# A hybrid decoder step: the gate tiles go through DRAM, and TensorE's order has their products earlier

## The chip, the cores and the metric

The kernel runs on one core of a Trainium2 chip. The core has TensorE (PE, matrix products into PSUM), VectorE (DVE), ScalarE (ACT), GpSimd (POOL) and SyncE (SP, which issues nearly all DMA transfers here). Each engine works through its own list of instructions in order; semaphores hold an instruction back until what it reads is there. The metric is the device time of one execution in microseconds (us); lower is better.

## What is computed

One layer of a decoder for 520 tokens (512 of a prompt and 8 samples), 1024 features, all in float32. Three branches stand side by side, each with a gate, and a feed-forward network follows:

```python
h = rms_norm(x, g_mix)
proj = h @ w_in                                  # 5632 columns
u_a, z_b, u_c, gate_in = proj[..., :1024], proj[..., 1024:2048], proj[..., 2048:2560], proj[..., 2560:]
y_a = rg_lru(causal_conv4(u_a))                  # branch A: two gates per block, a gated real recurrence
y_b = silu(layer_norm(causal_conv31(glu(z_b))))  # branch B: depthwise convolution of width 31
y_c = glu_c(gelu(s5_ssm(u_c)))                   # branch C: complex diagonal recurrence
g_a, g_b, g_c = split(sigmoid(gate_in + b_gate)) # 3 x 1024 columns
merged = g_a * (y_a @ w_pa) + g_b * (y_b @ w_pb) + g_c * (y_c @ w_pc)
x = x + merged @ w_out
x = x + swiglu(rms_norm(x, g_ffn) @ w_ffn_in) @ w_ffn_out     # width 2816
return rms_norm(x, g_final), the states of the branches
```

## The kernel before

Features lie on the 128 partitions and the 520 tokens on the free axis, as two halves of 260. A *column tile* is 128 output features. A large product takes both operands split into a high part and the remainder and adds up three products (`prod`, line 236, its matmuls on line 244): for one column tile over 1024 input features that is 8 x 3 x 2 = 48 matmuls of 260 tokens, over 512 input features 24. The weights of a column tile are fetched by SyncE in pairs of tiles (`wload`, line 205, two buffers `wraw`), ScalarE makes the high part (`whi`, line 216), and VectorE or GpSimd the remainder (`wlo`, line 217); the set `ON_POOL` names the pieces that go to GpSimd. `whi` and `wlo` have two buffers each, and the products' PSUM tiles `mm` three.

TensorE's order is written out by hand in `ORDER` (line 43) as a list of steps with the number of a tile; the program calls the steps in this order, and everything that a step does on the other engines is put into their lists by a scheduler at build time. Instructions of ScalarE that need a function table (sigmoid, tanh, exp, sqrt, gelu, silu; `tact`) keep the order of the program among themselves. The steps that matter here:

- `b0.t`, `b1.t`: the two halves of branch B's input (w_in columns 12 + t and 8 + t); `bc.t`: the convolution of width 31 for one of four tiles (`b_conv`), 30 instructions on VectorE's line 1176 that each add one tap. They have low priority, so VectorE's other work goes ahead of them, and the first of them is kept behind the instruction that `marks[3]` names: the end of the fourth S5 recurrence (line 907).
- `cp`, `cq`, `cr`, `cd`, `cm`, `ci`, `co` with tile 0 to 3: the S5 branch. `cp` and `cq` make coefficients on VectorE and GpSimd, `cr` transposes them, `cd` and `cm` make the products inside a chunk of four tokens, `ci` multiplies the inputs and runs the recurrence (scans on VectorE, with GpSimd's help), `co` makes the output. Their tiles come from a pool `hp` of 8 buffers.
- `a.t`, `ac.t`, `ag.t`, `ar.p`: branch A: input product, convolution of width 4, the two block gates (with small weights `w_rg`, `w_ig`, line 1066), and the recurrence of a pair of tiles; `asp` splits its results.
- `gelu`, `glu.t`: the end of branch C.
- `gc.c`, `ga.c`, `gb.c`: column tile c of the gate of branch C, A, B (`gate`, 48 matmuls and a sigmoid).
- `pc.c`, `pa.c`, `pb.c`: the projections (`proj`; `pc` and `pb` have 24 matmuls, `pa` 48). VectorE multiplies the product by the gate (line 1245) and adds it to the merged tile (line 1247).
- `lnp`, `ln1`, `ln2`, `ln3`: branch B's layer norm. `lnp` adds up the four convolved tiles (lines 1191 to 1193), `ln1` and `ln2` are column sums on TensorE (line 1187), `ln3` makes branch B's result, which `pb` needs.

A gate's result stays in SBUF until its projection: a `q` tile holds four column tiles, there are 11 buffers of this kind (`qp`), and the gates take six of them; the merged tile is the gate tile of branch C itself. `t` tiles (`tp`, 17 buffers of one column tile) serve for everything that lives shortly.

After `pb.7` come the output projection (8 column tiles), the feed-forward network and the final norm.

Of the kernel before, what the change touches and what calls it, by code (L numbers as in the profile page):

```python
"""One step of the hybrid decoder: parallel RG-LRU / Conformer / S5 mixers, gated merge, SwiGLU FFN.

Layout: features on partitions, the 520 tokens (512 prompt + 8 samples) on the free axis as two halves of
[256 prompt | 4 samples].  Large products run on TensorE in float32r with both operands split exactly into a
12-bit high part and the remainder (hi*hi + hi*lo + lo*hi, accumulated in float32).  The S5 recurrence runs over
chunks of four tokens: chunk inputs and the outputs inside a chunk are small float32 products, and the recurrence
over chunks is a real scan in a frame that rotates with the state.
"""
# [17 lines left out]
P = 128  # L26
NT = 520
# [16 lines left out]
bs b0.0 cp.0 as b0.1 ct s0 cp.1 ap b1.0 cr.0 b0.2 b1.1 cd.0 cq.1 ci.0 cr.1 b0.3 b1.3 cm.0 cq.0 ci.1 a.0 a.1 a.2  # L44
ac.0 cd.1 cp.2 co.0 cq.2 ac.1 cm.1 a.3 cr.2 ag.0 co.1 cd.2 ag.1 ac.2 ar.0 b1.2 ci.2 a.4 a.5 ac.3 cm.2 cp.3 gc.0
gc.1 cr.3 co.2 cd.3 ag.2 cq.3 cm.3 ci.3 ag.3 bc.0 ac.4 ar.1 gc.2 gc.3 ac.5 a.6 co.3 ag.4 ag.5 bc.1 ar.2 a.7 bc.2
gc.4 bc.3 gelu gc.5 ac.6 gc.6 ag.6 glu.0 glu.1 gc.7 ac.7 glu.2 glu.3 ga.0 ag.7 ar.3 asp pc.0 ga.1 pc.1 pc.2 pc.3
pc.4 pc.5 ga.2 ga.3 ga.4 pc.6 pc.7 ga.5 gb.0 lnp pa.0 pa.1 gb.1 pa.2 pa.3 pa.4 ga.6 pa.5 ga.7 pa.6 ln1 gb.2 gb.3
ln2 pa.7 ln3 gb.4 gb.5 pb.0 pb.1 gb.6 gb.7 pb.2 pb.3 pb.4 pb.5 pb.6 pb.7
# [4 lines left out]
def hybrid_step(ctx: ExitStack, tc, a, o):  # L54
# [13 lines left out]
    def eng(key):  # L68
        """Vector or GpSimd, by piece of work."""
        return G if key in ON_POOL else V  # L70
# [55 lines left out]
    def table(func):  # L126
        """Loads func's table where the order of the table functions, which is the order here, needs it."""
        if SETS[func] != last_tab[1]:
            last_tab[0] = after(S.preload_act_table_set(SETS[func]), last_tab[0])  # L129
            last_tab[1] = SETS[func]  # L130

    def tact(out, x, func, **kw):
        """An activation that needs a table."""
        table(func)
        last_tab[0] = after(S.activation(out, x, func, **kw), last_tab[0])  # L135

    # ------------------------------------------------------------------ constants, first loads
# [66 lines left out]
    # ------------------------------------------------------------------ weights: load, split  # L204
# [17 lines left out]
    def wcol(src, key, c, nk, k0=0, pair=True, dst=None):  # L222
        """hi, lo of column tile c of src, rows k0*128 on; columns come in pairs."""
# [10 lines left out]
    def prod(ps, w, xk, first=True, last=True):  # L234
        """ps[:, h, :260] += w.T @ x ; w=(hi, lo) [P, nk, P]; xk = list of (hi, lo) [P, 520]."""
# [14 lines left out]
    # ------------------------------------------------------------------ x: statistics, transposes, h  # L250
    # the order of each engine up to the first products
# [5 lines left out]
    # ------------------------------------------------------------------ scalars of the S5 recurrence  # L257
    def exp_acc(out, x, shape, sl, E=V):
        """exp to float32's accuracy: 2^k times a polynomial."""
# [78 lines left out]
    # Transposed rows.  The first half of the tokens goes ahead: its statistics, its h and its products of four  # L338
    # feature tiles come before the rows of the second half are there.
# [3 lines left out]
    # four feature tiles of a half of the tokens in two banks each  # L343
# [18 lines left out]
    def rstd_of(sl):  # L362
        """1/rms of the columns sl of ss, from the sums of squares."""
# [5 lines left out]
    RS = (0, 1, 3, 4)  # columns of the prompt's row tiles in ss and rstd; 2 is the samples'  # L369
# [9 lines left out]
    def x_copy4(h, k, e):  # L379
        """Feature tiles k, k+1 of a half."""  # L380
        dst, src = xT[0][:, k:k + 2, h * HN:h * HN + 256], ph4[h][:, k:k + 2, :]
        seq(e, S.activation(dst, src, AF.Copy) if e == "s" else V.tensor_copy(dst, src))
# [213 lines left out]
    # powers a^1..a^4: pw[:, ri, s, k]  # L596
# [17 lines left out]
    # q = (a - 1) / lambda  # L614
# [15 lines left out]
    # unit phase of four steps, |a|^4  # L630
# [8 lines left out]
    # ------------------------------------------------------------------ branch C: S5  # L639
    # udein[:, ct]: [8 samples | j=0 | j=1 | j=2 | j=3 | 8 samples], token 4m+j at (j, m)  # L640
# [23 lines left out]
    # tables of the phase: v1[:, ri, s, b] = e^{i phi b}, b < 16 ; v2[:, ri, s, c] = e^{i phi 16 c}, c < 8  # L664
# [7 lines left out]
    def powers(tab, n, br, bi):  # L672
        """tab[.., 0..n) = powers of (br, bi); leaves base^n in (br, bi)."""
# [17 lines left out]
    def unit(r, i):  # L691
        """One Newton step to modulus 1."""
# [12 lines left out]
    # discretised B: bb[:, ri, s, c]  # L705
# [9 lines left out]
    def c_tr():  # L715
        """C transposed to [(q p), s, c] and with the two groups of a state tile side by side (imaginary negated)."""
# [13 lines left out]
    # initial states of the samples, [(q p), ri, s, b]  # L730
# [15 lines left out]
    def c_pool(ct):  # L746
        """Coefficients of state tiles 4ct..4ct+3 that no token enters."""
# [32 lines left out]
        # phases e^{i phi m} over the 128 chunks  # L780
# [23 lines left out]
    def c_pool2(ct):  # L804
        """C a^{j+1}, the outputs' coefficients."""
# [27 lines left out]
    def c_prep(ct):  # L833
        """Transposed input coefficients, the products inside a chunk, the tokens by chunk."""
# [11 lines left out]
        # rows (k, c): token 4m + 3 - k of channel c; samples in front as k=3, behind as k=0  # L846
# [9 lines left out]
    def c_prod(ct):  # L856
        """Products inside a chunk, transposed and shifted by output."""
# [21 lines left out]
    def c_in(ct):  # L879
        """Chunk inputs, then the recurrence over the chunks."""  # L880
# [36 lines left out]
        # samples: a s0 + input  # L917
# [12 lines left out]
    def h_pairs(n):  # L930
        """(hi, lo) of 2n tiles."""
# [50 lines left out]
    # ------------------------------------------------------------------ branch A: RG-LRU  # L982
# [3 lines left out]
    fin_a = cst.tile([P, 160], F32, name="fin_a")  # (k t) 24 last prompt inputs | (b t) 64 new sample inputs | t 8 | (b t) 64  # L986

    def a_states():
# [14 lines left out]
        # -8 softplus(-lam) = -8 (max(-lam, 0) + log1p(exp(-|lam|)))  # L1003
# [5 lines left out]
        # log1p(e) = 2 atanh(e / (2 + e))  # L1009
# [72 lines left out]
    def a_rec(pair):  # L1082
        """Gated recurrence of channel tiles 2 pair, 2 pair + 1."""
# [11 lines left out]
        for t in ts_:  # L1095
# [5 lines left out]
            # samples  # L1101
# [21 lines left out]
    # ------------------------------------------------------------------ branch B: Conformer convolution  # L1123
    gext = [qt([P, 2, 1096]) for _ in range(2)]
    fin_b = cst.tile([P, 152], F32, name="fin_b")  # (k t) 120 | (b t) 32
# [101 lines left out]
    # ------------------------------------------------------------------ gates, projections  # L1227
    gt = {}

    def gate(br, c):  # L1230
        if c % 4 == 0:
            gt[br, c // 4] = qt([P, 4, NT])
# [3 lines left out]
        tact(hv(gt[br, c // 4][:, c % 4, :]), ev(ps), AF.Sigmoid, bias=vb("b_gate", 8 * br + c))  # L1236

    mx = []

    def proj(br, wname, nk, xk, c):  # L1240
        w = wcol(a[wname][0], wname, c, nk)
        ps = mm()
        prod(ps, w, xk)
        m, g = gt[2, c // 4][:, c % 4, :], gt[br, c // 4][:, c % 4, :]
# [322 lines left out]
```

## Time and profile before

| | us |
|---|---|
| median of 3 runs | 943.51 |
| lowest and highest run | 942.85, 944.31 |
| the profiled execution, first to last instruction (span) | 940.4 |
| TensorE busy in it | 864.3 |
| VectorE busy | 609.5 |
| ScalarE busy | 347.6 |
| GpSimd busy | 289.5 |

The page gives the profiled execution's span; what lies around it is taken from the runs. Its instructions are told by engine, line of the kernel, operation and tiles ("out<-in"); "x8" counts instructions; an entry in brackets is time in which the engine stood before them, with the instruction that ended the wait.

### The profile page before, as it was taken

The numbers are of one execution on the slowest core, as the hardware profiler recorded it, in microseconds if no ns is written. First come the engines' busy times: TensorE is split into PE (matmuls) and PEld (weight loads), VectorE is DVE, ScalarE is ACT, GpSimd is POOL, SyncE is SP. The second block draws the span as 40 slices with busy tenths as digits, with TensorE's granted clock in tenths as the row PEclk, the third lists the DMA queues.
The fourth block names the chain that finished last, engine by engine and source line by source line (L and its number), as shares of the span: only waits on it lengthen the run. The fifth ranks groups of instructions, "written<-read, shape, count | busy, mean of one in ns | idle before, by whom it ended". The sixth has DMA issues, their size and how long they took to land.

```text
span 940.4 us, 17346 instructions
## 1 busy us (share of the span) xinstructions
PE 864.3 (92%) x7329; PEld 853.8 (91%) x7329; DVE 609.5 (65%) x942; ACT 347.6 (37%) x516; POOL 289.5 (31%) x363
## 2 busy tenths in 40 slices
PE   6888767957798799999999999999999999999997
PEld 5887767957798699999999999999999999999997
DVE  7899695889999999993546454444442244444453
ACT  6522234627484623223634342333321222223331
POOL 6569994648674441242121210000000000000021
PEclk9998998979799899999999999999999999999999
DMA  6814212130202032222226223333123432321232
GB/s 195 262 57 136 68 51 64 45 114 1 68 24 90 24 133 91 90 91 90 75 72 232 95 85 101 121 100 99 41 84 90 145 98 91 112 91 43 84 99 91
DMA packets 97756, 87.99 MB, mean 94 GB/s; under 512 B 7923, under 2 KB 95207, under 8 KB 97151
## 3 DMA queue, kind: packets, MB, share of 16 engines
q1 hardware_dynamic: 97343, 86.28, 28.3%
q8 instruction: 57, 0.93, 0.4%
q0 software_dynamic: 320, 0.57, 0.2%
q14 instruction: 20, 0.16, 0.1%
q10 hardware_dynamic: 16, 0.03, 0.0%
HBM read 81.23 MB, written 6.19 MB: 93 GB/s over the span
## 4 chain that ended last, share of the span: by engine, by line
PE 61%; DVE 12%; issue 1%; ACT 1%; DVEq 0%
PE mm L244 57%; DVE q L1176 4%; PE mm L1516 3%; DVE t L1176 2%; DVE h L248 1%; DVE wlo L217 1%; DVE q L1109 1%; ACT t L135 0%; DVE tx L1040 0%; DVE t L574 0%; DVE q L1110 0%; DVE q L1245 0%; PE ms L1356 0%; DVE t L1098 0%; PE mm L1187 0%
## 5 line engine op out<-in xcount | busy, mean ns | idle before, releaser
L244 PE MATMUL mm<-q,whi 128*128 128x260 f32 x3296 | 534.3, 284 | 1.6 <-ACT whi L216 1.6
L244 PEld LDWEIGHTS mm<-q,whi 128*128 128x128 f32 x3296 | 454.8, 190 | 2.0 <-ACT whi L216 1.8
L244 PE MATMUL mm<-q,wlo 128*128 128x260 f32 x1648 | 333.1, 283 | 10.1 <-DVE wlo L217 7.1
L216 ACT ACTIVATE whi<-wraw 128x1024 fp32r<-128x1024 f32 (+3 forms) x146 | 139.5, 956 | 433.1 <-PE mm L244 367.9
L244 PEld LDWEIGHTS mm<-q,wlo 128*128 128x128 f32 x1648 | 255.8, 190 | 12.0 <-DVE wlo L217 8.4
L217 DVE TENSOR_TENSOR wlo<-wraw,whi 128x1024 fp32r<-128x1024 f32 (+3 forms) x113 | 127.3, 1127 | 49.4 <-ACT whi L216 49.1
L244 PE MATMUL mm<-h,whi 128*128 128x260 f32 x800 | 130.9, 286 | 2.6 <-DVE h L248 2.5
L1388 POOL TENSOR_TENSOR t<-t,t 128x260 f32<-128x260 f32 (+1 forms) x9 | 8.8, 976 | 369.3 <-ACT t L1386 369.3
L244 PEld LDWEIGHTS mm<-h,whi 128*128 128x128 f32 x800 | 111.5, 191 | 3.1 <-DVE h L248 2.7
L217 POOL TENSOR_TENSOR wlo<-wraw,whi 128x1024 fp32r<-128x1024 f32 (+1 forms) x33 | 71.7, 2173 | 129.5 <-ACT whi L216 114.0
L244 PE MATMUL mm<-h,wlo 128*128 128x260 f32 x400 | 82.0, 287 | 6.3 <-DVE wlo L217 6.0
L244 PEld LDWEIGHTS mm<-h,wlo 128*128 128x128 f32 x400 | 62.7, 192 | 6.9 <-DVE wlo L217 6.4
L1176 DVE SCALAR_TENSOR_TENSOR q<-q,vec 128x512 f32<-128x512 f32 x60 | 59.1, 985 | 1.2
L1467 DVE TENSOR_TENSOR t<-mm,t 128x520 f32<-128x520 f32 x22 | 15.4, 699 | 67.4 <-PE mm L244 58.3
L1457 DVE TENSOR_TENSOR t<-mm,t 128x520 f32<-128x520 f32 x22 | 15.4, 700 | 63.4 <-PE mm L244 63.4
L129 ACT ACT_TABLE_LOAD x23 | 29.5, 1283 | 1.1 <-PEq L1555 0.7
L1176 DVE SCALAR_TENSOR_TENSOR t<-q,vec,t 128x512 f32<-128x512 f32 x30 | 28.4, 945 | 0.4
L1482 DVE TENSOR_TENSOR q<-mm,q 128x520 f32<-128x520 f32 x12 | 8.4, 698 | 27.9 <-PE mm L244 27.9
L1307 POOL TENSOR_TENSOR t<-t,t 128x520 f32<-128x520 f32 x7 | 12.4, 1770 | 41.7 <-ACT t L1306 41.7
L1176 DVE SCALAR_TENSOR_TENSOR q<-q,vec,q 128x512 f32<-128x512 f32 x30 | 24.3, 810 | 0.8
L1245 DVE TENSOR_TENSOR q<-mm,q 128x520 f32<-128x520 f32 x24 | 16.6, 690 | 12.1 <-PE mm L244 12.1
L135 ACT ACTIVATE t<-t,zero_t 128x520 f32<-128x520 f32 x30 | 21.2, 719 | 0.0
(422 smaller groups left out, 1001.8 us busy)
## 6 DMA issues: line engine op xcount, KB each, us to landing
wraw<-w_ffn_in SPq DMA_DIRECT2D x22, 1024.0 KB
wraw<-w_in SPq DMA_DIRECT2D x21, 1024.0 KB
wraw<-w_ffn_out SPq DMA_DIRECT2D x16, 384.0 KB
wraw<-w_ffn_out SPq DMA_DIRECT2D x16, 320.0 KB
wraw<-w_pa SPq DMA_DIRECT2D x4, 1024.0 KB
wraw<-w_out SPq DMA_DIRECT2D x4, 1024.0 KB
xT_d<-q SPq DMA_DIRECT2D x2, 1040.0 KB
q<-xT_d SPq DMA_DIRECT2D x2, 1040.0 KB
```

Source lines behind the costliest of these rows:

```text
L129: last_tab[0] = after(S.preload_act_table_set(SETS[func]), last_tab[0])
L135: last_tab[0] = after(S.activation(out, x, func, **kw), last_tab[0])
L216: S.activation(hi, raw, AF.Copy)
L217: e.tensor_tensor(lo, raw, hi.bitcast(F32), op=ALU.subtract)
L244: T.matmul(ps[:, h, 0:HN], w, x[:, h * HN:(h + 1) * HN], start=first and i == 0, stop=last and i == 2)
L248: e.tensor_tensor(lo, src, hi.bitcast(F32), op=ALU.subtract)
L1176: ins = V.scalar_tensor_tensor(pv(acc), win(k), wdw(k, t), pv(acc), op0=ALU.mult, op1=ALU.add)
L1245: V.tensor_tensor(hv(g), ev(ps), hv(g), op=ALU.mult)
L1307: G.tensor_tensor(ssum, ssum, sq, op=ALU.add)
L1457: V.tensor_tensor(hv(sl), ev(ps), hv(R2), op=ALU.mult)
L1467: V.tensor_tensor(hv(up), ev(ps), hv(R2), op=ALU.mult)
L1516: T.matmul(ps[:, 0, 0:HN], w[:, k, :], x[:, h * HN:(h + 1) * HN], start=j == 0 and k == 0 and i == 0, stop=j == 1 and k == hk - 1 and i == 2)
```

## The change

Each gate tile is now written to DRAM as soon as its sigmoid is done, and the tile's buffer is a `t` tile. Each projection first fetches gate tiles until three are in SBUF or under way, in the order of their use. The merged tile is a `q` tile of its own, taken by the projections of branch C. `ORDER` is another one: the gate products stand in pairs among the branches' steps, from after `b0.3` on; `b1.2` stands before `b1.3`, and the projections `pa` come four before and four after `ln1` and `ln2`.

The other lines of the diff take comments and docstrings away.

```diff
 ORDER = """
-bs b0.0 cp.0 as b0.1 ct s0 cp.1 ap b1.0 cr.0 b0.2 b1.1 cd.0 cq.1 ci.0 cr.1 b0.3 b1.3 cm.0 cq.0 ci.1 a.0 a.1 a.2
-ac.0 cd.1 cp.2 co.0 cq.2 ac.1 cm.1 a.3 cr.2 ag.0 co.1 cd.2 ag.1 ac.2 ar.0 b1.2 ci.2 a.4 a.5 ac.3 cm.2 cp.3 gc.0
-gc.1 cr.3 co.2 cd.3 ag.2 cq.3 cm.3 ci.3 ag.3 bc.0 ac.4 ar.1 gc.2 gc.3 ac.5 a.6 co.3 ag.4 ag.5 bc.1 ar.2 a.7 bc.2
-gc.4 bc.3 gelu gc.5 ac.6 gc.6 ag.6 glu.0 glu.1 gc.7 ac.7 glu.2 glu.3 ga.0 ag.7 ar.3 asp pc.0 ga.1 pc.1 pc.2 pc.3
-pc.4 pc.5 ga.2 ga.3 ga.4 pc.6 pc.7 ga.5 gb.0 lnp pa.0 pa.1 gb.1 pa.2 pa.3 pa.4 ga.6 pa.5 ga.7 pa.6 ln1 gb.2 gb.3
-ln2 pa.7 ln3 gb.4 gb.5 pb.0 pb.1 gb.6 gb.7 pb.2 pb.3 pb.4 pb.5 pb.6 pb.7
+bs b0.0 cp.0 as b0.1 ct s0 cp.1 ap b1.0 cr.0 b0.2 b1.1 cd.0 cq.1 b0.3 gc.0 gc.1 ci.0 cr.1 b1.2 cm.0 cq.0 b1.3 a.0 ci.1
+a.1 a.2 ac.0 cd.1 cp.2 co.0 cq.2 ac.1 a.3 gc.2 gc.3 cm.1 cr.2 ag.0 co.1 cd.2 ag.1 ac.2 ar.0 ci.2 a.4 a.5 ac.3 cm.2
+cp.3 gc.4 gc.5 cr.3 co.2 cd.3 ag.2 cq.3 cm.3 gc.6 gc.7 ci.3 ag.3 bc.0 ac.4 ar.1 ga.0 ga.1 ac.5 a.6 co.3 a.7 ga.2 ga.3
+ag.4 ag.5 bc.1 ar.2 bc.2 ga.4 ga.5 bc.3 gelu ac.6 ga.6 ga.7 ag.6 glu.0 glu.1 ac.7 gb.0 gb.1 glu.2 glu.3 ag.7 ar.3 asp
+gb.2 gb.3 pc.0 pc.1 pc.2 pc.3 pc.4 pc.5 gb.4 gb.5 pc.6 pc.7 lnp pa.0 pa.1 pa.2 pa.3 ln1 gb.6 gb.7 ln2 pa.4 pa.5 pa.6
+pa.7 ln3 pb.0 pb.1 pb.2 pb.3 pb.4 pb.5 pb.6 pb.7
 """
...
+    g_d = dr.tile([3, 8, P, NT], F32, name="g_d")
     gt = {}
 
     def gate(br, c):
-        if c % 4 == 0:
-            gt[br, c // 4] = qt([P, 4, NT])
         w = wcol(w_in, "in", 20 + 8 * br + c, 8)
         ps = mm()
         prod(ps, w, hx)
-        tact(hv(gt[br, c // 4][:, c % 4, :]), ev(ps), AF.Sigmoid, bias=vb("b_gate", 8 * br + c))
-
-    mx = []
+        g = tt()
+        tact(hv(g), ev(ps), AF.Sigmoid, bias=vb("b_gate", 8 * br + c))
+        Y.dma_start(g_d[br, c], g)
+
+    mx, mg = [], {}
+    ahead = [(br, c) for br in (2, 0, 1) for c in range(8)]
 
     def proj(br, wname, nk, xk, c):
+        while ahead and len(gt) < 3:
+            n = ahead.pop(0)
+            gt[n] = tt()
+            Y.dma_start(gt[n], g_d[n[0], n[1]])
+        if br == 2 and c % 4 == 0:
+            mg[c // 4] = qt([P, 4, NT])
         w = wcol(a[wname][0], wname, c, nk)
         ps = mm()
         prod(ps, w, xk)
-        m, g = gt[2, c // 4][:, c % 4, :], gt[br, c // 4][:, c % 4, :]
-        V.tensor_tensor(hv(g), ev(ps), hv(g), op=ALU.mult)
+        m, g = mg[c // 4][:, c % 4, :], gt.pop((br, c))
+        V.tensor_tensor(hv(m if br == 2 else g), ev(ps), hv(g), op=ALU.mult)
         if br != 2:
             V.tensor_tensor(m, m, g, op=ALU.add)
         if br == 1:
             if c % 4 == 0:
-                gt["h"], gt["l"] = qt([P, 4, NT], F32R), qt([P, 4, NT], F32R)
-            mx.append((gt["h"][:, c % 4, :], gt["l"][:, c % 4, :]))
+                mg["h"], mg["l"] = qt([P, 4, NT], F32R), qt([P, 4, NT], F32R)
+            mx.append((mg["h"][:, c % 4, :], mg["l"][:, c % 4, :]))
             split(m, *mx[c])
```

## Rows read from the trace of the kernel before

**Rows 1.** The page: span, and busy time of each engine (share, instructions).

```profile
span 940.4 us, 17346 instructions
PE 864.3 (92%) x7329; PEld 853.8 (91%) x7329; DVE 609.5 (65%) x942; ACT 347.6 (37%) x516; POOL 289.5 (31%) x363
```

**Rows 2.** Windows: length, busy per engine (instructions), then TensorE's clock, DMA share, GB/s.

```profile
20.00:40.00 20.00, 18.29 (x146) 17.46 (x145) 16.45 (x58) 11.13 (x24) 13.36 (x15) 1.00 0.85 247
...
81.90:211.96 130.06, 96.75 (x993) 94.07 (x989) 105.31 (x143) 46.49 (x78) 93.17 (x132) 0.88 0.24 76
211.96:230.10 18.14, 15.67 (x130) 15.25 (x128) 17.95 (x21) 11.82 (x16) 15.68 (x17) 1.00 0.00 1
230.10:422.40 192.30, 171.82 (x1419) 169.25 (x1420) 188.28 (x219) 87.65 (x120) 87.14 (x71) 0.94 0.23 75
422.40:501.20 78.80, 78.80 (x653) 78.56 (x652) 42.35 (x52) 35.97 (x48) 17.36 (x10) 1.00 0.32 109
```

**Rows 3.** Waits of TensorE, 81.9 to 211.96: total us, times, longest.

```profile
PE ms L876 <- DVE t L866: 12.3, 1, 12.3
PE ms L841 <- DVE h L771: 9.1, 1, 9.1
PE mm L887 <- POOL h L849: 9.1, 2, 4.8
PE mm L244 <- POOL wlo L217: 2.5, 2, 1.5
```

**Rows 4.** Waits of TensorE, 212 to 501.2.

```profile
PE mm L244 <- DVE wlo L217: 12.9, 6, 6.0
```

**Rows 5.** VectorE's groups, 230.1 to 422.4: busy us, mean ns, idle before.

```profile
L1176 DVE SCALAR_TENSOR_TENSOR q<-q,vec 128x512 f32<-128x512 f32 x60 | 59.1, 985 | 1.2
L1176 DVE SCALAR_TENSOR_TENSOR t<-q,vec,t 128x512 f32<-128x512 f32 x30 | 28.4, 945 | 0.4
L1176 DVE SCALAR_TENSOR_TENSOR q<-q,vec,q 128x512 f32<-128x512 f32 x30 | 24.3, 810 | 0.8
L217 DVE TENSOR_TENSOR wlo<-wraw,whi 128x1024 fp32r<-128x1024 f32 (+1 forms) x16 | 17.9, 1119 | 0.0
```

**Rows 6.** Timeline of VectorE: start us, duration us, instruction.

```profile
230.08 1.64 DVE L907 TENSOR_TENSOR h<-h 128x512 f32<-128x512 f32 x1
...
419.17 0.74 DVE L1176 SCALAR_TENSOR_TENSOR q<-q,vec 128x512 f32<-128x512 f32 x1
...
421.72 0.70 DVE L1193 TENSOR_TENSOR t<-t,t 128x520 f32<-128x520 f32 x1 [1.20 <-POOL t L1192]
```

**Rows 7.** The chain that ended last: start us, us, what.

```profile
367.41 68.69 PE mm L244 x572
436.10 0.88 PE mm L1187 x4
436.97 11.48 PE mm L244 x96
...
449.33 103.73 PE mm L244 x864
```

**Rows 8.** Timeline of TensorE around the step `ci.0`.

```profile
81.30 0.64 PE L863 MATMUL ms<-h,q 128*32 128x128 f32 x16
86.28 4.00 PE L887 MATMUL mm<-h,h 128*128 128x136 f32 x16 [4.33 <-POOL h L849]
```

**Rows 9.** Timeline of TensorE after a wait of 6.00 us.

```profile
328.36 1.07 PE L244 MATMUL mm<-h,whi 128*128 128x260 f32 x4
...
330.87 0.64 PE L244 MATMUL mm<-h,whi 128*128 128x260 f32 x4
```

**Rows 10.** DMA issues: KB each, median us from issue to landing.

```profile
t<-state_cfm_conv POOLq DMA_DIRECT2D x2, 240.0 KB, 3.7
```

**Rows 11.** Waits of SyncE's queue: total us, times, longest.

```profile
SPq L209 <- DVE wlo L217: 546.4, 73, 31.2
...
SPq L1066 <- POOL t L924: 22.0, 1, 22.0
```

## The prediction

> **What bounds the kernel now.** The page comes first: over the span TensorE is busy 92% and VectorE 65% [rows 1], so TensorE looks like the bound everywhere. The windows by stage then show three different stages [rows 2]. From 81.9 to 212 us, where the S5 steps run, no engine is full: TensorE has 96.75 us of 130.06 at a granted clock of 0.88 (a mean of stretches at 2.4 and at 1.2 GHz), VectorE 105.31, GpSimd 93.17. From 230.1 to 422.4 VectorE has 188.28 of 192.30 us and TensorE 171.82. From 422.4 on TensorE is never idle until the last few microseconds, and its clock is 1.00. So the 76 us in which TensorE is idle (940.4 less 864.3) lie almost all ahead of 422.
>
> The waits of TensorE in the S5 stage name single late results: the table for `cm.1` (12.3 us), the coefficients for `cr.3` (9.1), the two token tiles of `ci.0` and `ci.1` (9.1 together), and GpSimd's weight splits (2.5) [rows 3]. In the next stage 12.9 us are six waits for VectorE's splits [rows 4].
>
> VectorE's own order shows why its stage has a fixed length. The depthwise convolution, 120 instructions of line 1176 with 59.1 + 28.4 + 24.3 = 111.8 us [rows 5], is held back until the last S5 recurrence has passed line 907, at 230.08; its last instruction is at 419.17, and the sum that `ln1` needs is done at 421.72 + 0.70 = 422.4 [rows 6]. Between these two points VectorE stands still only 4 us, so the 192.3 us are work. TensorE reaches `ln1` at 436.10, 13.7 us later, and the chain of waits is TensorE from 367.41 on [rows 7].
>
> **Which engine decides.** By the rows of the whole span, filling TensorE's idle time could give up to 76 us; by the rows of the stage from 230 to 422 the time comes back only as far as VectorE's work ends earlier, or as TensorE has less to do after `ln1`. The Trainium skill (Perfetto Trace Analysis, Identifying the Most-Contended Engine) says that the engine with the highest occupancy is the one to optimize; for the whole span that names TensorE and would give the first rival below, for the stage it names VectorE, whose work this change leaves as it is. I take the stage, since its 98% stands beside TensorE's 89% there [rows 2].
>
> **The change, part by part.**
>
> *The end of the chain, after `ln1`.* Before, these products follow `ln1`: `gb.2` to `gb.7`, `pa.7`, `pb.0` to `pb.7`. Afterwards they are `gb.6`, `gb.7`, `pa.4` to `pa.7`, `pb.0` to `pb.7`. A product over 8 feature tiles has 48 matmuls; two take 11.48 us [rows 7], so 5.74 each, and one over 4 tiles 2.87. Before, `pb.7` ends at 449.33 plus 432 of the 864 matmuls in 103.73 us, 51.87: 501.2. Afterwards `ln1` to `pb.7` is 0.88 + 11.48 + 0.88 + 4 x 5.74 + 8 x 2.87 = 59.2 us. If `ln1` could start at 422.4, when VectorE has its sum now, `pb.7` would end at 481.6: 19.6 us earlier. Everything behind it (output projection, FFN, 439 us) is untouched and TensorE-bound, so this passes through whole.
>
> *VectorE's list between the S5 recurrence and `ln1`.* The splits of `gc.5`, `gc.6`, `gc.7` leave it and those of `gb.2`, `gb.4`, `gb.5`, `ga.7` enter it: one more at 1.12 us [rows 5]; the two instructions behind `pa.4` leave it, some 1.4 us. Net -0.3 us, taken as nothing: VectorE is full there, so nothing would cover it.
>
> *When that list starts.* Call d the delay of VectorE's list; the gain is 19.6 - d. Six more products (`gc.2` to `gc.7`) now stand between `cd.0` and `ci.3`, 34.4 us. TensorE's busy time of that stretch becomes 96.75 + 34.4 = 131.2 us at the clock of before, or down to 119.6 if every matmul ran at the full clock (12% of 96.75 less); I take 125, near the middle, since fewer gaps keep the clock up but some stay. Of the waits, those of `ci.0` and `ci.1` (9.1) are covered by `b0.3`, `gc.0`, `gc.1` and `b1.3`, `a.0` set ahead of them; that of `cm.1` (12.3) by `gc.2`, `gc.3` (11.5). That of `cr.3` (9.1) keeps the cover that it had, and GpSimd's splits (2.5) stay. So `ci.3` starts some 125 + 11.6 = 136.6 us after 81.9 where it took 130.06: 6.5 us late. VectorE uses part of the wait for instructions of the convolution of branch A, which stand between the recurrence's own at 215 to 230 now; that stretch is full (17.95 of 18.14 [rows 2]). I take d = 4. Its bounds: -24.8, if all of VectorE's idle time from 81.9 to 212 (130.06 - 105.31) were filled; +24, below.
>
> *The order inside the S5 stage.* Now `ci.0` waits 4.33 us after `cd.0` at 81.30 [rows 8]; afterwards three products, 17.2 us, stand there, so `ci.0` comes 12.9 us later, and every buffer of that S5 tile is freed later. And `gc.6`, `gc.7` stand directly before `ci.3`, 11.5 us in which its inputs are ready. If nothing in between caught up, d would be 24.4. I count on catching up, as VectorE itself was idle for 24.8 us in this stretch and TensorE waited 12.3 and 9.1 us for it.
>
> *TensorE standing before `ln1`.* It now gets there first. After a wait of 6.00 us at 327.76 four matmuls took 1.07 instead of 0.64 us for about 3 us [rows 9]: 1.4 us to add.
>
> *Stores and loads.* 24 stores and 24 loads of 260 KB (128 x 520 x 4 bytes), 12.8 MB on 88; one weight load of 1 MB goes, as `b1.2` now comes before `b1.3` and both share a pair. The nearest transfer, 240 KB, took 3.7 us to land [rows 10]. Three tiles are fetched ahead, 8.6 us of the shortest products, so a load is there in time: nothing is added. Without that cover a late tile would hold VectorE and the split queued behind it. After 422 the 16 DMA engines are 32% busy at 109 GB/s [rows 2]; 12 loads and 2 stores, 3.7 MB in 59 us, add 63 GB/s: about half busy. On SyncE's queue each store waits for its sigmoid with weight loads behind it; but these are for two pairs later, and SyncE spends 546.4 us waiting for buffers anyway [rows 11]. At the worst each load after `ln1` delays the weights behind it by its own transfer, 260 KB at 247 GB/s or 1.1 us (an estimate from the stretch 20 to 40 us [rows 2]): 13 us.
>
> *Buffers.* Two wide `q` tiles at a time are held for the gates instead of six; that frees memory and no time. Each gate takes one of 17 `t` buffers until its store has landed, some 4 us by the same row [rows 10]. That these are scarce is seen: SyncE stood 22.0 us for one, for `w_rg` [rows 11]. It is part of the slower rival.
>
> Sum: 19.6 - 4 - 1.4 = 14.2 us. The profiled span 940.4 becomes 926.2. The median of the runs, 943.5, lies 3.1 above the span: 929.3, say **929**.
>
> **The rivals.**
>
> *TensorE stays the bound (0.17).* The gate products fill the gaps and the S5 steps run no later or earlier, so that VectorE's list starts 5 to 25 us sooner: gain 23 to 43, 900 to 920, middle 912. For it: VectorE's 24.8 idle us before 212. Against: the waits at `ci` and `cr` hang on GpSimd and on buffers of the S5 tiles, which the change doesn't speed up.
>
> *The S5 chain is held up (0.13, slower).* Both delays, 12.9 at `ci.0` and 11.5 at `ci.3`, arrive at line 907 whole: d = 24.4, gain 19.6 - 24.4 - 1.4 = -6.2: 950. It decides from d = 18.2 on. For it: each S5 step is one link of a single chain through four engines; against: those idle times.
>
> *Queue and buffers (0.06).* The loads in front of weights cost their 13 us, or a `t` buffer is late: gain about 1, 942 to 946.
>
> *Same (0.06).* d between 16.3 and 20, anywhere among these.
>
> **How the numbers follow.** The forecast (d from -3 to 15: 922 to 940 us) has 0.58, the other cases as above. Faster than by 0.2% (1.9 us, about what a measurement tells from no change): 0.58 + 0.17 + 0.02 = 0.77; within it 0.06; slower 0.17. The range goes from 909, below which a third of the first rival lies, to 947, above which most of the slower one lies, with 0.15 outside in all; the forecast's own is 922 to 940.
>
> **What would show it.** Right: the sigmoids of the gates are spread from 95 us on; TensorE's waits for `cm.1`, `ci.0` and `ci.1` go; line 907 of the last recurrence is at 228 to 240; the convolution still ends 189 us after it; TensorE waits for VectorE just before `ln1`, or in late splits ahead of it; `pb.7` ends 59 us after `ln1`, near 486. Wrong: `ci.3` 20 us late, the convolution's 192 us much shorter or longer, loads that VectorE waits for in the last products, or idle TensorE after `ln1`.

## The result: 0.8% slower, and the profile after

The changed kernel takes 951.19 us (median of 4 runs, 949.04 to 953.12) where the kernel before, run beside it, takes 943.61 (942.85 to 944.31). The ratio is 1.008, 95% interval 1.0062 to 1.0098. The forecast was 929 with a range of 909 to 947: wrong in its sign, and outside the range. The profiled execution took 952.3 us.

The page after, with the span and each engine's busy time, answers to [rows 1]:

```profile
span 950.5 us, 17472 instructions
PE 875.8 (92%) x7329; PEld 862.9 (91%) x7329; DVE 600.1 (63%) x942; ACT 346.2 (36%) x515; POOL 284.9 (30%) x363
```

The span has grown by 10.1 us. TensorE has the same 7329 matmuls and is busy 11.5 us longer; its idle time is 74.7 us where it was 76. So the loss is not more waiting in sum, and that is the first thing to explain.

The windows after, cut at the events that cut [rows 2] (`ci.3`, line 907 of the last recurrence, the sum for `ln1`, the end of `pb.7`); columns as there:

```profile
81.90:239.68 157.78, 134.78 (x1277) 130.48 (x1278) 105.35 (x149) 55.70 (x90) 92.74 (x133) 0.92 0.26 81
239.68:258.81 19.13, 15.67 (x130) 15.26 (x128) 16.92 (x16) 14.69 (x19) 18.04 (x16) 1.00 0.22 70
258.81:442.20 183.39, 153.94 (x1234) 151.22 (x1235) 177.42 (x212) 80.83 (x112) 77.63 (x69) 0.90 0.33 107
442.20:509.60 67.40, 67.26 (x553) 66.60 (x552) 45.52 (x54) 30.20 (x41) 19.50 (x11) 1.00 0.47 160
```

The S5 stage is 27.7 us longer: 134.78 us of TensorE work, where 125 were counted on, and 23.0 us idle, where 11.6 were. VectorE has the same 105 us of work in it as before and now stands idle for 52.4 us. The next stage is 9 us shorter. Then the timeline at the three points that the prediction hung on, VectorE first, TensorE's `ln1` last:

```profile
258.81 0.73 DVE L907 TENSOR_TENSOR h<-h 128x512 f32<-128x512 f32 x1
...
439.27 2.90 DVE L1193 TENSOR_TENSOR t<-t,t 128x520 f32<-128x520 f32 x1
...
449.21 1.04 PE L1187 MATMUL mm<-t,ones_t 128*128 128x260 f32 x4
```

Line 907 is 28.7 us later than before, the sum (442.17) 19.8, `ln1` 13.3, the end of `pb.7` 8.4, the end of the span 10.1.

**TensorE's own account.** Windows from 81.9 us to `ln1`, from there to the end of `pb.7`, and to the end; first the kernel before, then the changed one:

```profile
81.90:435.94 354.04, 297.78 (x2653) 292.12 (x2650) 316.45 (x384) 148.71 (x216) 195.99 (x219) 0.92 0.22 72
435.94:501.20 65.26, 65.26 (x540) 65.02 (x539) 37.44 (x46) 33.22 (x45) 17.36 (x10) 1.00 0.34 115
501.20:940.40 439.20, 433.01 (x3623) 432.38 (x3621) 187.05 (x245) 130.12 (x180) 21.71 (x17) 1.00 0.29 95
```

```profile
81.90:449.21 367.31, 311.40 (x2697) 303.97 (x2697) 302.23 (x378) 152.28 (x220) 188.42 (x217) 0.92 0.30 95
449.21:509.60 60.39, 60.25 (x495) 59.59 (x493) 42.99 (x51) 29.14 (x40) 19.50 (x11) 1.00 0.47 162
509.60:950.50 440.90, 434.05 (x3619) 432.82 (x3619) 186.49 (x244) 129.20 (x179) 22.04 (x17) 0.99 0.30 94
```

Idle ahead of `ln1`: 354.04 - 297.78 = 56.3 us before, 367.31 - 311.40 = 55.9 after. Busy from 81.9 to the end of `pb.7`: 363.0 before, 371.7 after, for the same matmuls. The 8.4 us at `pb.7` are these 8.6 us; 1.7 us more come behind it, where four weight transfers of the FFN now stand in the chain of waits (not followed further).

**What the waits are for.** TensorE's waits from 81.9 us to `ln1` on line 244 (the products), before and after; the last row shown of the changed kernel is the S5 step `cr.3`:

```profile
PE mm L244 <- DVE wlo L217: 13.1, 7, 6.0
PE mm L244 <- DVE t L248: 5.1, 1, 5.1
PE mm L244 <- POOL wlo L217: 3.2, 4, 1.5
...
PE mm L244 <- ACT whi L216: 1.6, 1, 1.6
```

```profile
PE mm L244 <- POOL wlo L217: 17.7, 5, 6.5
PE mm L244 <- DVE wlo L217: 13.9, 5, 5.9
PE mm L244 <- DVE t L248: 6.9, 2, 6.0
PE mm L244 <- ACT whi L216: 4.8, 3, 3.1
PE mm L244 <- ACT t L247: 4.4, 3, 2.5
PE ms L841 <- DVE h L771: 2.8, 1, 2.8
```

The waits on S5 steps, 30.5 us before [rows 3], are down to 5.6; the forecast had left the 9.1 before `cr.3`. The waits in products, 25.7 us before, are now 50.1. Of these 24.4 us more, 14.5 lie in the S5 stage (17.2 after, 2.7 before) and 9.9 behind it. So one kind of wait was exchanged for the other. A reading that fits: a product set into an S5 gap needs two halves of its weights, which ScalarE and then VectorE or GpSimd make while they are busy with the same S5 step.

**What the busy time is.** Before, a few long waits (12.3, 9.1); after, 20 of 0.8 us or more where there were 12. Behind such a wait TensorE runs at the lower of its two levels for a while, 1.2 instead of 2.4 GHz: behind a wait of 6.55 us that ended at 388.00, the granted clock is 0.51 until 393.2 and 1.00 from 393.5 on, and a matmul of 260 columns starts every 0.217 us instead of every 0.12. The timeline of the changed kernel there:

```profile
388.00 0.80 PE L244 MATMUL mm<-h,wlo 128*128 128x260 f32 x2 [6.55 <-POOL wlo L217]
388.60 1.07 PE L244 MATMUL mm<-h,whi 128*128 128x260 f32 x4
...
393.49 0.64 PE L244 MATMUL mm<-h,whi 128*128 128x260 f32 x4
```

Adding up the timeline's rows of 260-column matmuls whose mean step is over 0.15 us (0.1196 at the full clock) between 81.9 us and 60 us past `ln1`: 37.9 us before, of which 14.2 are lost to the rate; 65.5 after, of which 27.1 are lost. These sums also take in the tail of a row that stands before a wait; counted matmul by matmul (steps of 0.15 to 0.27 us) the loss is 11.0 us before and 22.7 after. By either count it has grown by 12 to 13 us. The busy time has grown by only 8.6, since the small matmuls of the S5 steps, which ran at the lower level behind the long waits, got 5.1 us shorter (30.8 to 25.7). The largest such group, `ci`, before and after, with busy us, mean ns, idle before:

```profile
L887 PE MATMUL mm<-h,h 128*128 128x136 f32 x64 | 11.8, 358 | 9.1 <-POOL h L849 9.1
```

```profile
L887 PE MATMUL mm<-h,h 128*128 128x136 f32 x64 | 8.1, 279 | 0.0
```

The mean granted clock from 81.9 us to `ln1` is 0.92 in both kernels (the windows above): the low level now falls on more matmuls and on less idle time.

### The profile page after: what moved, and what is told of

Its sections match the earlier page's. It is cut to its first block, busy times and chain, and to the rows that moved or that the text cites. A ratio compares the mean times of both kernels' runs of the same rounds, so it can differ in the third digit from the quotient of the medians.

```text
span 950.5 us, 17472 instructions
## 1 busy us (share of the span) xinstructions
PE 875.8 (92%) x7329; PEld 862.9 (91%) x7329; DVE 600.1 (63%) x942; ACT 346.2 (36%) x515; POOL 284.9 (30%) x363
## 5 line engine op out<-in xcount | busy, mean ns | idle before, releaser
L244 PE MATMUL mm<-q,whi 128*128 128x260 f32 x3296 | 542.9, 288 | 3.5 <-ACT whi L216 3.3
L244 PEld LDWEIGHTS mm<-q,whi 128*128 128x128 f32 x3296 | 463.2, 193 | 4.9 <-ACT whi L216 3.7
L244 PE MATMUL mm<-q,wlo 128*128 128x260 f32 x1648 | 338.8, 287 | 25.1 <-DVE wlo L217 13.9
L244 PEld LDWEIGHTS mm<-q,wlo 128*128 128x128 f32 x1648 | 260.6, 193 | 27.2 <-DVE wlo L217 15.2
L244 PE MATMUL mm<-h,wlo 128*128 128x260 f32 x400 | 81.9, 287 | 6.7 <-POOL wlo L217 6.5
L1176 DVE SCALAR_TENSOR_TENSOR q<-q,vec 128x512 f32<-128x512 f32 x60 | 55.5, 925 | 2.3 <-ACT q L1174 1.2
L135 ACT ACTIVATE t<-mm,vec 128x520 f32<-128x520 f32 x44 | 29.9, 685 | 22.9 <-PE mm L244 14.3
L244 PE MATMUL mm<-t,t 128*128 128x260 f32 x96 | 17.6, 340 | 12.7 <-DVE t L248 6.9
L244 PEld LDWEIGHTS mm<-t,t 128*128 128x128 f32 x96 | 15.2, 233 | 14.6 <-DVE t L248 7.5
L1176 DVE SCALAR_TENSOR_TENSOR t<-q,vec,t 128x512 f32<-128x512 f32 x30 | 27.7, 924 | 0.7
L1176 DVE SCALAR_TENSOR_TENSOR q<-q,vec,q 128x512 f32<-128x512 f32 x30 | 27.6, 921 | 0.6
L1491 DVE TENSOR_TENSOR q<-mm,q 128x520 f32<-128x520 f32 x12 | 8.4, 699 | 27.7 <-PE mm L244 27.7
```

The costliest lines, as they stand in the source:

```text
L244: T.matmul(ps[:, h, 0:HN], w, x[:, h * HN:(h + 1) * HN], start=first and i == 0, stop=last and i == 2)
L1176: ins = V.scalar_tensor_tensor(pv(acc), win(k), wdw(k, t), pv(acc), op0=ALU.mult, op1=ALU.add)
L1491: V.tensor_tensor(xc, ev(ps), xc, op=ALU.add)
```

## The experiments

All are compared with the kernel before, run beside them. Busy and idle are TensorE's from 81.9 us to `ln1`, in the profiled execution; L907 is that of the last recurrence, sum the end of line 1193. The kernel before took 943.61 to 944.33 us beside these runs. A changed order of TensorE, another kind of buffer or another order inside a product also lets the scheduler put the other engines' instructions in another order: matched by the order of their source lines in the traces, 146 of VectorE's 942 stand elsewhere in e11 than in the changed kernel, 130 in e12 than in the kernel before, 28 in f1 than in e11, and only 2 in f4 than in the kernel before. Most differences below hold such a part too.

| run | median us | ratio, 95% | L907 | sum | ln1 | busy | idle |
|---|---|---|---|---|---|---|---|
| before | 943.61 to 944.33 | | 230.1 | 422.4 | 435.9 | 297.8 | 56.3 |
| after | 951.19 | 1.0062 to 1.0098 | 258.8 | 442.2 | 449.2 | 311.4 | 55.9 |
| e1_old_order | 949.52 | 1.0045 to 1.0072 | 229.2 | 417.0 | 441.5 | 298.8 | 60.8 |
| e2_ci0 | 953.05 | 1.0073 to 1.0103 | 264.7 | 450.9 | 451.2 | 312.6 | 56.6 |
| e3_ci3 | 949.81 | 1.0044 to 1.0070 | 241.7 | 427.6 | 446.8 | 311.9 | 52.9 |
| e4_both | 958.77 | 1.0143 to 1.0171 | 248.6 | 432.5 | 456.8 | 316.0 | 58.9 |
| e5_no_dram | 951.10 | 1.0053 to 1.0077 | 258.8 | 438.6 | 449.2 | 311.3 | 56.0 |
| e6_before_half_taps | 941.23 | 0.9957 to 0.9980 | 230.6 | 349.0 | 434.6 | 299.2 | 53.5 |
| e7_after_half_taps | 943.58 | 0.9979 to 1.0001 | 258.2 | 414.1 | 438.4 | 309.6 | 46.9 |
| e8_tp21 | 949.73 | 1.0035 to 1.0067 | 257.7 | 445.0 | 448.5 | 310.4 | 56.3 |
| e9_old_tp21 | 952.43 | 1.0083 to 1.0111 | 231.3 | 419.0 | 443.7 | 300.7 | 61.1 |
| e10_splits_dve | 951.53 | 1.0080 to 1.0111 | 258.1 | 434.8 | 447.7 | 308.7 | 57.1 |
| e11_after_hi_first | 941.87 | 0.9975 to 0.9992 | 251.0 | 435.7 | 440.6 | 304.0 | 54.7 |
| e12_before_hi_first | 942.55 | 0.9982 to 1.0000 | 233.9 | 424.8 | 433.8 | 296.8 | 55.1 |
| f1_fill_cr3 | 935.61 | 0.9902 to 0.9929 | 246.4 | 429.3 | 430.9 | 302.0 | 47.0 |
| f2_fill_all | 940.77 | 0.9956 to 0.9981 | 247.5 | 430.5 | 438.8 | 307.7 | 49.2 |
| f3_old_no_dram | 963.10 | 1.0190 to 1.0218 | 232.3 | 415.1 | 456.1 | 306.9 | 67.2 |
| f4_before_warm | 944.41 | 0.9999 to 1.0016 | 232.2 | 424.5 | 438.0 | 310.9 | 45.3 |
| f5_after_warm | 955.39 | 1.0093 to 1.0127 | 261.5 | 434.5 | 458.8 | 340.0 | 36.9 |

**Is it the S5 chain, held up at `ci.0` and `ci.3`?** The time after is that of the slower rival, 950, so its mechanism was tried first: the order undone, and each of the two steps moved.

```diff
e1 (ORDER of before; a gate is fetched ahead only once stored)
-        while ahead and len(gt) < 3:
+        while ahead and len(gt) < 3 and ahead[0] in done_g:
e2, e4 (ORDER, the part that differs)
-cd.0 cq.1 b0.3 gc.0 gc.1 ci.0
+cd.0 cq.1 ci.0 b0.3 gc.0 gc.1
e3, e4 (ORDER, the part that differs)
-cm.3 gc.6 gc.7 ci.3
+cm.3 ci.3 gc.6 gc.7
```

> Half of the change alone: the gates go through DRAM, TensorE's order is that of before. Theory A (the new order holds the S5 chain back): the last L907 is near 230 us again and the time is that of before, 941 to 946. Theory B (the stores and loads, their buffers and SyncE's queue cost the time): 949 to 953, with L907 near 230 and waits for weights or for t tiles after it.

> The changed kernel with ci.0 set ahead of b0.3, gc.0, gc.1 again. Theory A: ci.0 starts near 87 instead of 104.23 us, the 17 us pass on to the last L907 (242 instead of 258.81), and the time falls to 934 to 938. Rival (the chain of S5 steps has slack there, so that ci.0's delay would have been caught up, and only the products right ahead of ci.3 count): L907 at 255 or later, 947 to 951. Theory B: 949 to 953.

> The changed kernel with ci.3 set ahead of gc.6, gc.7. Theory A: ci.3 starts 9 to 11 us sooner (229 instead of 239.68), L907 near 249, the time 940 to 943. Rival (the inputs of ci.3 are late, and it would only wait): ci.3 at 236 or later with a TensorE wait in front, 948 to 951. Theory B: 949 to 953.

> The changed kernel with both moves. Theory A: the two delays add, the last L907 is at 230 to 234, the sum for ln1 near 415 to 420, and the time 922 to 928. Rival C (TensorE itself becomes the bound ahead of ln1: it has 311 us of work between 81.9 and 449.2 and waits for late splits): L907 as early as that, but ln1 10 to 20 us behind VectorE's sum, 933 to 942. Theory B: 945 to 953.

Theory A fell. With `ci.0` back at 85.78 us, `ci.1` comes at 132.13 (126.27 after) and the last line 907 later than ever. The timeline of e2:

```profile
85.78 2.64 PE L887 MATMUL mm<-h,h 128*128 128x136 f32 x10 [4.30 <-POOL h L849]
...
132.13 2.02 PE L887 MATMUL mm<-h,h 128*128 128x136 f32 x16
...
264.68 0.73 DVE L907 TENSOR_TENSOR h<-h 128x512 f32<-128x512 f32 x1
```

And where line 907 did come early it did not help. In e3 `ci.3` starts 11.9 us sooner than in the changed kernel (227.78), line 907 comes 17.1 us sooner, `ln1` 2.4, and the time is within the noise of that of the changed kernel. In e1 line 907 is at 229.21, the sum is done 5.5 us earlier than before, and `ln1` starts 5.5 us later:

```profile
229.21 1.64 DVE L907 TENSOR_TENSOR h<-h 128x512 f32<-128x512 f32 x1
...
414.06 2.89 DVE L1193 TENSOR_TENSOR t<-t,t 128x520 f32<-128x520 f32 x1
...
441.45 0.82 PE L1187 MATMUL mm<-t,ones_t 128*128 128x260 f32 x3
```

In e1, e3 and e4 TensorE reaches `ln1` 24, 19 and 24 us after the sum. That is rival C's mechanism in all three, and more of it than its 10 to 20 us, so its times (933 to 942) were missed: TensorE's own list arrives last. It does so in every run of the table, by 0.3 us in e2 and 1.6 in f1, with no wait in front of `ln1` in these two. Why e4 is slower than e3 by 9 us is open; its waits for branch A's high parts (line 247) are 10.7 us where the changed kernel has 4.4.

**Is it VectorE's list at all?** Half of the convolution's taps are left out, in the kernel before and in the changed one.

```diff
-        for k in range(1, 31):
+        for k in range(1, 16):
```

> The kernel before with 15 of the 30 later taps of the branch B convolution, 56 us less for VectorE; the other taps are left out of the result. Theory V, the prediction's (VectorE's list sets ln1, TensorE is only late by what is placed in front): the sum for ln1 56 us earlier, near 366, and all the 56 idle us of TensorE ahead of ln1 could close: 905 or below. Theory T: TensorE reaches ln1 10 to 20 us earlier at most, since only its 20.5 us of waits between 230 and 436 hang on VectorE's splits: 922 to 938, with ln1 over 40 us behind the sum.

> The changed kernel with the same 15 taps left out. Theory T: it has 10 waits, 31 us, between 259 and ln1, most for splits queued behind taps; with the taps gone it gains more than the kernel before does, 15 to 25 us: 926 to 936. If the waits of this order come from elsewhere (t buffers, DMA, GpSimd), it gains under 10: 942 or more.

The timeline of e6, VectorE's sum and TensorE's `ln1`:

```profile
348.28 0.70 DVE L1193 TENSOR_TENSOR t<-t,t 128x520 f32<-128x520 f32 x1 [1.44 <-POOL t L1192]
...
434.59 1.04 PE L1187 MATMUL mm<-t,ones_t 128*128 128x260 f32 x4
```

The sum is 73 us earlier and `ln1` 1.4 us: theory V, on which the forecast stood, is refuted. The gain, 0.3%, is even under theory T's range. In the changed kernel the same cut gains 0.8%, more than in the kernel before; its idle time falls by 9 us (in the profiled execution, 940.3 us, the fastest of its ten), and it still is no faster than the kernel before with all its taps. That is 7.6 us, short of what theory T had said (15 to 25): the waits for VectorE's low parts fell from 13.9 to 8.5 us, and those for GpSimd's still are 12.6, so most of its waits are not for VectorE's taps.

**Is it the traffic, or the buffers?**

```diff
e5 (and f3, with the ORDER of before)
-        Y.dma_start(g_d[br, c], g)
...
-            Y.dma_start(gt[n], g_d[n[0], n[1]])
...
-        V.tensor_tensor(hv(m if br == 2 else g), ev(ps), hv(g), op=ALU.mult)
+        V.tensor_tensor(hv(g), ev(ps), ones_t[:, 0:1].unsqueeze(1).to_broadcast([P, 2, HN]), op=ALU.mult)
e8 (and e9, with the ORDER of before, through DRAM)
-    qp = ctx.enter_context(tc.tile_pool(name="qp", bufs=11))
+    qp = ctx.enter_context(tc.tile_pool(name="qp", bufs=10))
...
-    tp = ctx.enter_context(tc.tile_pool(name="tp", bufs=17))
+    tp = ctx.enter_context(tc.tile_pool(name="tp", bufs=21))
```

> The changed kernel in its order, but no gate is stored or loaded; the products are multiplied by a constant, so the gates are left out of the result (the gate products and sigmoids are still made). After the first runs theory A (the S5 chain sets the end by the last L907) has failed: with L907 back at 229 us the old order with DRAM still took 949.5. Theory B (stores, loads and t buffers cost some 6 us in either order): 943 to 946. Theory T (TensorE's own list sets ln1, and its waits and the slow clock behind them make the time, whatever the traffic): 949 to 953, with 50 to 58 us of TensorE waits between 81.9 us and ln1.

> The changed kernel with 21 t buffers instead of 17, paid for with one q buffer (10 instead of 11). Theory B in its form of scarce t buffers: the waits for RG-LRU tiles (t) and for gate loads shorten and the time falls by 3 to 6 us, to 945 to 948. Theory T: the order and the waits for splits stay, 949 to 953.

> The order of before, gates through DRAM, 21 t buffers and 10 q buffers. It asks where the 5.5 us of the old order with DRAM went, as without stores and loads the new order is no faster (traffic by itself is free). If the gates' t tiles crowd out the tiles of branch A (waits of TensorE for L247 and L248, 5.0 and 1.5 us there), they go: 943 to 946. If the cause is SyncE's queue, weights behind stores that wait for a sigmoid: 948 to 951, and the same waits.

> The order of before, with no gate kept at all: neither stored nor loaded, the products multiplied by a constant (the gates are left out of the result; gate products and sigmoids are still made, into t tiles). The old order with DRAM took 949.5. If the transfers and SyncE's queue make its 5.5 us: 943 to 945. If it is the orders of VectorE and ScalarE, which come out otherwise as soon as the gates lie in t tiles (150 and 66 of their instructions stand elsewhere than before): 948 to 951.

In the new order 12.8 MB of stores and loads cost nothing that can be measured: without them `ln1` is at 449.21 us, to the hundredth. Theory B is out there. Four more `t` buffers gained some 0.3% in the new order (the interval overlaps that of the changed kernel) and lost 3 us in the old. In the old order the kernel without any transfer is not faster but slower than with them, 963.1 to 949.5, outside both expectations. What e1 and f3 share is that the scheduler, given other tiles, put VectorE's and ScalarE's lists in another order. One place where this is seen in f3's timeline: ten taps (line 1176) stand in VectorE's list ahead of the multiplication of one projection (line 1250), and a product of a later projection waits 7.72 us for it:

```profile
402.54 9.98 DVE L1176 SCALAR_TENSOR_TENSOR q<-q,vec 128x512 f32<-128x512 f32 x10
412.44 1.30 DVE L1250 TENSOR_TENSOR t<-mm,ones_t 128x520 f32<-128x520 f32 x2
...
413.28 0.99 PE L244 MATMUL mm<-h,whi 128*128 128x260 f32 x3 [7.72 <-DVE t L1250]
```

That the lists' order is the cause in e1 and in f3 is argued, not shown: no run had the old lists with the gates in `t` tiles. f3 as a whole is 2% slower than the kernel before, more than the change itself; the wait shown is the one part of it that was traced.

**Is it the late splits?** Two ways to have the low part in time: GpSimd's nine splits of gate weights to VectorE, or all matmuls of the high part ahead of those of the low part.

```diff
e10 (the set ON_POOL, the part that differs)
-w.in.21 w.in.23 w.in.26 w.in.31 w.in.35 w.in.37 w.in.38 w.in.39 w.in.4 w.in.40 w.in.7
+w.in.4 w.in.7
e11 (changed kernel), e12 (kernel before)
-        for k, (xh, xl) in enumerate(xk):
-            prod1(ps, hi[:, k, :], lo[:, k, :], xh, xl, first and k == 0, last and k == n - 1)
+        seq3 = [(hi[:, k, :], x) for k in range(n) for x in xk[k]] + [(lo[:, k, :], xk[k][0]) for k in range(n)]
+        for i, (w, x) in enumerate(seq3):
+            for h in range(2):
+                T.matmul(ps[:, h, 0:HN], w, x[:, h * HN:(h + 1) * HN],
+                         start=first and i == 0, stop=last and i == len(seq3) - 1)
```

> The changed kernel with the nine weight splits of gate columns that GpSimd makes (2.4 to 2.9 us each) given to VectorE (1.12 us each). Theory S (in the new order the gate products stand in pairs between S5 steps, and their weight splits come late on the engine that is busy with the S5 step): the waits for GpSimd's splits fall from 17.7 us to under 8, the time to 940 to 947. Rival (the splits are late because of what both engines do, and VectorE's will be late instead): waits for VectorE's splits rise by as much, 949 to 954.

> The changed kernel with every product's 32 matmuls of the high part set ahead of the 16 of the low part, so that the low part is needed 3.8 us later in each product of 8 tiles. Theory S: of the 31.6 us of waits for low parts (10 pieces, longest 6.5 us) some 22 us go, and with them part of the slow clock behind each: 918 to 930. Rival (the waits for splits only show when the engines behind fall short of work time, and the wait moves to the high part of the next product, whose buffer comes free no sooner): 942 to 950.

> The kernel before with the same order inside each product. It has 16.3 us of waits for low parts, of which 12 go, and the waits on S5 steps (30.5 us) stay. Theory S: 928 to 936, so that the changed order, which has exchanged S5 waits for split waits, ends ahead of it by 5 us or more. Rival: 940 to 946, no different from the kernel before.

e10 went by its rival: the waits for GpSimd's splits fell from 17.7 to 4.0 us and those for VectorE's rose from 13.9 to 27.1. e11 took back the whole loss, 951.2 to 941.9; e12 gained only 0.1%. So with the low parts needed later the two orders are within 0.1% of each other, and late low parts are the likely cause of what the new order lost. They are not isolated, as the other engines' lists changed too. The size was not that of theory S in either run: e11's time, 941.87, lies just under the rival's range and e12's inside it. The waits for low parts did go,

```profile
PE ms L843 <- DVE h L773: 11.4, 1, 11.4
...
PE mm L241 <- DVE wlo L217: 5.4, 4, 3.0
...
PE mm L241 <- POOL wlo L217: 2.1, 2, 1.2
```

(e11's waits, where line 241 is the product), 31.6 to 7.5 us, but TensorE then stood 11.4 us before `cr.3` instead of 2.8, and its idle time is nearly the same, 54.7. What fell is its busy time, 311.4 to 304.0, and the part lost to the slow rate, 27.1 to 13.5 us (22.7 to 13.2 matmul by matmul).

**Can a wait be covered for good?**

```diff
f1 (e11's kernel, ORDER, the part that differs)
-gc.4 gc.5 cr.3 co.2 cd.3 ag.2 cq.3 cm.3 gc.6 gc.7 ci.3
+gc.4 gc.5 gc.6 gc.7 cr.3 co.2 cd.3 ag.2 cq.3 cm.3 ci.3
f2 (f1, and)
-ga.2 ga.3 ag.4 ag.5 bc.1 ar.2 bc.2 ga.4 ga.5 bc.3 gelu ac.6 ga.6 ga.7 ag.6 glu.0 glu.1 ac.7 gb.0 gb.1
+ga.2 ga.3 ga.4 ga.5 ag.4 ag.5 bc.1 ar.2 bc.2 bc.3 gelu ac.6 ga.6 ga.7 gb.0 gb.1 ag.6 glu.0 glu.1 ac.7
```

> The changed kernel with the high parts first in each product (941.9 us), and gc.6, gc.7 moved from in front of ci.3 to in front of cr.3, where TensorE waits 11.4 us for VectorE's coefficients. Theory W (each wait of TensorE is for one late result, and a product whose weights are there covers it): the wait at cr.3 falls below 2 us, ci.3 comes no later, and the time falls by 6 to 12, to 930 to 936. Rival P (the engines behind the S5 steps set the pace, and the wait comes back at the next step): TensorE's waits between 81.9 us and ln1 sum up as before, 58 us, and the time is 939 to 944.

> The same, with ga.4, ga.5 set ahead of ag.4 and gb.0, gb.1 ahead of ag.6, where TensorE waits 9.9 and 7.6 us for branch A's tiles. Theory W: 917 to 927. Rival P: 936 to 944, with those waits again at the next RG-LRU or projection step.

f1 is the fastest kernel here, 935.6 us, 0.85% ahead of the kernel before: the wait at `cr.3` is gone and `ci.3` comes 6.7 us sooner (theory W). Its timeline, the second line being `cr.3`:

```profile
208.84 5.61 PE L241 MATMUL mm<-q,whi 128*128 128x260 f32 x32 [4.34 <-ACT t L135]
...
216.21 1.03 PE L843 MATMUL ms<-ident,h 128*128 128x128 f32 x8
...
225.60 1.75 PE L889 MATMUL mm<-h,h 128*128 128x136 f32 x10 [3.02 <-DMA h<-ud_d]
```

Part of it came back: 4.34 us in the products set there, for a PSUM tile that a sigmoid still reads, and 3.02 at `ci.3`. f2 went by the other theory: the same trick at `ag.4` and `ag.6` lost 5 us again. TensorE's waits for branch A's high parts (line 249) rose from 7.8 to 13.4 us. A reading that fits both, from one run each: a wait can be covered where its result is late for a reason of its own; where the engine that makes it is behind, it comes back.

**Is it the clock?** Matmuls of no use keep TensorE busy in the waits.

```diff
f4 (kernel before, ORDER, the parts that differ; dm.n is n matmuls into a PSUM tile of their own)
-ac.1 cm.1
+ac.1 dm.60 cm.1
-gc.1 cr.3
+gc.1 dm.40 cr.3
f5 (changed kernel, ahead of ten products)
+    WARM = {"b0.3": 24, "a.3": 6, "gc.2": 14, "gc.3": 38, "gc.4": 32, "a.6": 24, "ag.4": 60, "ga.6": 18, "gb.0": 46, "pc.0": 50}
...
```

> The kernel before, with 60 matmuls of no use ahead of cm.1 and 40 ahead of cr.3, into a PSUM tile that nobody reads, 7.2 and 4.8 us at the full clock, in waits of 12.3 and 9.1 us; the other engines' orders are the same. If the clock that falls in a wait costs time behind it: the granted clock between 140 and 210 us is nearer 1.00, the time 1 to 3 us less, 941 to 943. If it costs nothing: 943.5 to 944.5, or more where the matmuls outlast the waits.

> The changed kernel, with matmuls of no use set ahead of the ten products that wait longest for a late split (312 in all, 37 us at the full clock, written to the product's own PSUM tile and overwritten by it), so that TensorE is busy in these waits. Some 100 of the other engines' 1,900 instructions stand elsewhere. Counting matmuls of 260 columns that ran at half rate between 81.9 us and ln1 + 60, the changed kernel lost 27.1 us to the slow clock, the one before 14.2, and f1 13.2. Theory K (short waits inside a stretch of products leave the slow clock to the products behind them, and that is the loss): the 27 us fall to 12 to 18 and the time to 938 to 945. Rival (the slow clock is a by-product and late splits set the pace, as in the S5 waits of the kernel before, where such matmuls gained nothing): 948 to 956.

Neither gained. Windows around the two steps (the granted clock is the third number from the end), in the kernel before and in f4:

```profile
140.00:150.00 10.00, 3.03 (x15) 3.03 (x16) 8.47 (x14) 2.58 (x5) 5.43 (x9) 0.51 0.52 159
200.00:210.00 10.00, 6.13 (x121) 5.37 (x121) 7.52 (x15) 2.03 (x4) 3.33 (x7) 0.61 0.52 161
```


```profile
140.00:150.00 10.00, 4.58 (x31) 4.40 (x30) 8.47 (x14) 2.15 (x4) 5.86 (x9) 0.76 0.57 158
200.00:210.00 10.00, 5.53 (x66) 4.58 (x68) 9.25 (x18) 1.60 (x3) 4.06 (x7) 0.83 0.36 113
```

The granted clock was 0.51 and 0.61 in the kernel before and rose to 0.76 and 0.83, and the time did not fall. That the steps behind these waits hang on other engines would explain it; no run tests that. In f5 the loss to the slow rate fell from 27.1 to 18.0 us, but of the 37.3 us of added matmuls only 19.0 went into waits (idle 55.9 to 36.9): the rest made TensorE later. 37.3 - 19.0 - 9.1 = 9.2 us; 9.6 were measured at `ln1` in the profiled execution, 960.5 us, the slowest of its five (the median is 4.2 us above that of the changed kernel). So the price of the clock behind the short waits is counted from the rows, not isolated: the run meant to isolate it bought it back at a higher price.

## Why the prediction was wrong, by its steps

- **"If `ln1` could start at 422.4, when VectorE has its sum now ... 19.6 us earlier": this step failed.** It took VectorE's list as what `ln1` waits for. TensorE was already 13.7 us behind the sum [rows 6, 7] (13.5 by the timeline, which has `ln1` at 435.94), and this was read as a lag that the new order would take away ("It now gets there first"). But the change sets work ahead of `ln1`, 5 us of it (65.3 to 60.3 us of work behind it), and TensorE gets to `ln1` by its own work and waits. e6 shows it: the sum 73 us earlier, `ln1` 1.4 us. TensorE would have been there first only with the covers for nothing: 435.9 + 5.0 - 21.4 us of waits covered is 419.5, an estimate from the prediction's own terms. Measured from 435.9 on are + 5.0 (moved work) + 8.6 (slower matmuls) - 24.9 (S5 waits gone) + 24.4 (new waits in products) = + 13.1; `ln1` came 13.3 later. The new waits and the slower matmuls are the terms that were left out. The stage's 98% for VectorE beside 89% for TensorE [rows 2] said which engine is fuller in this stage, not which is last at the step that both meet in. The Trainium skill (Perfetto Trace Analysis, Identifying the Most-Contended Engine) calls the engine with the highest occupancy the most contended one. Read over the whole span, where the prediction set it aside, that is TensorE (92%; VectorE 65%), and e6 agrees.
- **"When that list starts", d = 4.** It was 28.7, beyond its upper bound, for S5 work on TensorE took 134.8 us and its idle time 23.0. But d does not set the end: at d near 0 (e1) and at 18.5 (e4) the kernel takes 949.5 and 958.8. VectorE's list itself, taken as unchanged (-0.3 us), was 10.9 us shorter in busy time (188.3 to 177.4).
- **The covers.** The waits for `cm.1`, `ci.0`, `ci.1` did go, 25 us with that of `cr.3`: right (that of `cr.3` was forecast to stay). That the products put there are ready, unsaid in the prediction, was wrong: 24 us of waits for their own weights and inputs stand in their place.
- **"Fewer gaps keep the clock up".** There were more of them, shorter. In the S5 stage the mean granted clock did rise, 0.88 to 0.92, and TensorE's work there still was 134.8 us, above even the 131.2 that the prediction had for the clock of before; in the next stage the clock fell from 0.94 to 0.90. Over both it is 8.6 us more busy time for the same matmuls. The prediction had one case of it, 1.4 us.
- **After `ln1`**, 59.2 us forecast, 60.4 measured. **Stores and loads at nothing, buffers no time**: right in the new order (e5, e8). The old order with the gates in `t` tiles is 5.5 us slower with the transfers (e1) and 19 without (f3); that is open above.
- **The rival at 950** has the time by luck, with the wrong mechanism: undoing its two delays together (e4) made the kernel slower.

## What to carry to other kernels

Before work is moved behind a step where two engines meet, ask which of them comes last there, and cost that one's list: its work, its waits, and what each wait leaves behind it. Making the supposed bound lighter (half of the taps) answers that in one run. A product set into a gap is cover only if its own operands do not hang on the engines that made the gap; what helped here was to make its need later (high parts ahead of low parts), then to move it.

## What the runs showed that was not expected

- The same idle time, 56 us in both kernels, left 14.2 us lost at 1.2 GHz where it lay in 12 waits, some of them long, and 27.1 where it lay in 20, most of them inside stretches of products (11.0 and 22.7 matmul by matmul).
- Raising the granted clock from 0.51 to 0.76 and from 0.61 to 0.83 in two waits on S5 steps was worth nothing that can be measured (f4, ratio 0.9999 to 1.0016).
- 12.8 MB more of DMA traffic, 95 GB/s from 81.9 us to `ln1` instead of 69 without it (e5), cost nothing that can be measured in the new order.
- With TensorE's order unchanged and no transfer, the gates in `t` tiles and a constant in their place in the multiplication moved the time by 2% (f3).
